# Stick-breaking attention: element-wise steps of heads, z and the last sums go from VectorE to GpSimd in quarters, and the dense filler is spread over whole blocks

## The chip, the cores and the metric

The kernel runs on one core of one Trainium2 chip. A core has five engines with queues of their own: TensorE (PE, matrix products and transposes into PSUM), VectorE (DVE), ScalarE (ACT), GpSimd (POOL, which in this kernel works on SBUF only) and SyncE (SP, which here issues DMA transfers). The metric is device time in microseconds, as the median of several runs; before the change it is 2796.8 us (three runs, 2795.46 to 2797.88).

## The reference

Two layers over a sequence of 2048 tokens with 1024 channels, all in float32. Layer 0 mixes by trailing means, then keys and values are computed once. The change lies in layer 1, which for 16 heads of 64 channels does this:

```
q, z = split(rms_norm(x) @ b_w_in)              # q normed per head
logits = q . k / 8                               # s < t only
keep   = prod over s<j<t of (1 - sigmoid(logits[t, j]))
o[t]   = sum over s of sigmoid(logits[t, s]) * keep * v[s]
x = x + (o * silu(z)) @ b_w_out
x = x + (p @ ple_w) * sigmoid(x @ ple_gate_w)
```

The kernel uses that a weight is a difference of two neighbouring products of `1 - sigmoid`: it multiplies running products with differences of v, and adds a term for the end of the block (`ends`).

## The kernel before, in words

All dense products are made from pairs: each float32 operand is split into a high part (rounded to the matmul's type) and a low part (the rest), and three matmuls per product are summed (high·high, high·low, low·high). A low part is made by one subtraction, such as line 853.

The first part of the program (to line 734) does layer 0 and k, v, q for four chunks of 512 tokens. The second part is the attention and all of layer 1's dense products.

**Attention.** The work is cut into slots `(c, h, kc)`: query chunk c from 3 down to 0, head h from 0 to 15, key chunk kc from c down to 0. That is 64, 48, 32 and 16 slots for c = 3, 2, 1, 0; "block" means the slots of one c. A slot has four steps, one for each 128 queries (or 128 keys). At step n the code calls, in this order:

- `turn` for step n − 6: four TensorE transposes of the running products into a PSUM tile `psa` (two buffers, line 799), a cast to the high part on ACT (line 802) and the low part on DVE (line 803);
- `front` for step n: two matmuls for the logits (774, 775), `1 - sigmoid` on ACT (778), on diagonal slots a mask by `affine_select` on GpSimd (780), and the running product as a scan on DVE (785);
- the filler: so many pieces of dense work as `rate` has added up to, each piece one matmul and what follows it;
- `gather` for step n − 8: two matmuls with v (811, 812). At the last step of a head it also joins the head's two partition halves: an ACT copy of one half (816) and a DVE sum (817). After every second head, four ACT instructions add `ends` (823) and GpSimd multiplies the pair of heads by silu(z) (824).

**Filler.** While c = 3 runs, the filler is `gate_z` for all four chunks: eight products of 24 matmuls each, z's normalisation on DVE (873), a sigmoid on ACT (875), a product on GpSimd (876) and a store to DRAM. While c = 2, 1, 0 run, it is `post(c + 1)`: eight output products with the residual (897), ACT's high part (899) and GpSimd's low part (900), then eight gates with sigmoid (919), product (922) and two sums (923 on GpSimd, 924 on DVE), transposes back (929), a copy (931) and the store. `pair_up` makes the high and low part of a finished pair of heads (852, 853). `post(0)` has no attention beside it; it is the tail, where `tail[0]` is set.

The rate is such that the filler of a block (`POST` pieces) is spent before the block ends:

```
POST = 8 * 24 + 8 * 30 + 9
rate = POST / (64.0 * c3 - 2 * LAG_G)      # LAG_G = 8
```

What is left when the block's heads are all there is run at once. The written order is the order of priority; a planner, which has costs of its own for the instructions, sets the final order on each engine and can move an instruction behind later ones where it takes its inputs to be late. Each engine then executes its queue in order.

Of the kernel before, what the change touches and what calls it, by code (L numbers as in the profile page):

```python
# [29 lines left out]
def f(ap):  # L30
    return ap.bitcast(F32)
# [3 lines left out]
def trunk_kernel(ctx, tc, x, p, a_norm, a_w_in, a_w_group, a_scale, a_w_out, kv_norm, w_kv,  # L35
# [143 lines left out]
    with ExitStack() as st:  # L179
# [14 lines left out]
        def tmp(nm):  # L194
            return t2.tile([P, W5], F32, tag="tmp", name=nm, bufs=8)

        halo = [[cp.tile([P, HALO], F32, name=f"halo{o}_{i}") for i in range(2)] for o in range(KT)]
        for o in range(KT):
            V.memset(halo[o][0], 0.0)

# [536 lines left out]
    with ExitStack() as st:  # L737
# [68 lines left out]
        def gather(st, kt):  # L806
            cs = slice((kt if st["diag"] else 0) * P, W5)
            if st["diag"] and kt == 0:
                st["o"].append(pso.tile([P, W5], F32, tag="pso", name="pso"))
            po, at, vv = st["o"][0], st["at"].pop(kt), st["v"]  # L810
            T.matmul(po[:, cs], vv[:, kt, :], at[:, 0, cs], start=(st["diag"] and kt == 0), stop=False)  # L811
            T.matmul(po[:, cs], vv[:, kt, :], at[:, 1, cs], start=False, stop=(st["last"] and kt == 3))  # L812
            if st["last"] and kt == 3:
                half, os, c, h2 = st["h"] % 2, st["os"], st["c"], st["h"] // 2
                mine, other = slice(half * HD, (half + 1) * HD), slice((1 - half) * HD, (2 - half) * HD)
                A.copy(out=os[mine], in_=po[other])  # L816
                V.tensor_tensor(out=os[mine], in0=po[mine], in1=os[mine], op=ALU.add)  # L817
                if half:
                    zt = t2.tile([P, W5], F32, tag="zt", name="zt", bufs=1)
                    nc.sync.dma_start(out=zt, in_=zd[c][h2])  # L820
                    for j in range(4):
                        js = slice(j * P, (j + 1) * P)
                        A.activation(out=os[:, js], in_=os[:, js], func=AF.Identity, bias=ends[c][:, h2, j : j + 1])  # L823
                    G.tensor_tensor(out=os, in0=os, in1=zt, op=ALU.mult)  # L824
                    outs[c].append(os)

        tail = [0]

        def dense():
            if tail[0] and tail[0] % 4:  # L830
# [16 lines left out]
        def pair_up(c):  # L847

            if len(ogs[c]) < len(outs[c]):
                os = outs[c][len(ogs[c])]  # L850
                pr = pair("og")
                A.copy(out=pr[:, 0], in_=os)
                V.tensor_tensor(out=pr[:, 1], in0=os, in1=f(pr[:, 0]), op=ALU.subtract)
                ogs[c].append(pr)

        def gate_z(c):

            xs = chunk[c]["x2"] if c == NSUB - 1 else []
            for o in range(len(xs), KT):
                pr = pair("xz")  # L860
                nc.sync.dma_start(out=f(pr), in_=x2p[c][o])
                xs.append(pr)
            ps = (psl if "w" in early else psa).tile([P, 4, P], F32, tag="psl" if "w" in early else "psa", name="psar")
            for j in range(4):
                T.transpose(ps[:, j, :], r2s[c][:, j : j + 1].to_broadcast([P, P]), ident)
            rb = kap.tile([P, W5], F32, tag="rb", name="rb")
            A.copy(out=rb, in_=ps.rearrange("q j t -> q (j t)"))
            for o in range(KT):
                wz = early.pop("w") if "w" in early else stored(wzd[o])
                ps = dense()  # L870
                yield from piecewise(ps, wz, xs, 0)
                zr = t2.tile([P, W5], F32, tag="tmp", name="zr", bufs=4)
                V.tensor_tensor(out=zr, in0=ps, in1=rb, op=ALU.mult)
                sg = t2.tile([P, W5], F32, tag="tmp", name="sgz", bufs=4)
                A.activation(out=sg, in_=zr, func=AF.Sigmoid)
                G.tensor_tensor(out=zr, in0=zr, in1=sg, op=ALU.mult)
                nc.sync.dma_start(out=zd[c][o], in_=zr)
                if c == 0:
                    pair_up(NSUB - 1)

        POSTZ = 8 * 24
        POST = 8 * 24 + 8 * 30 + 9

        def post(c):

# [17 lines left out]
            for k in range(2):  # L903
# [9 lines left out]
            for o in range(KT):  # L913
                wg = stored(wgd[o])
                wl = stored(wld[o])
                ps = dense()
                yield from piecewise(ps, wg, x3, 0)
                sg = t2.tile([P, W5], F32, tag="tmp", name="sg", bufs=4)
# [4 lines left out]
                (V if tail[0] else G).tensor_tensor(out=sg, in0=sg, in1=f(x3[o][:, 1]), op=ALU.add)  # L923
                V.tensor_tensor(out=sg, in0=sg, in1=f(x3[o][:, 0]), op=ALU.add)

                def finish(o=o, sg=sg):
                    pt = psa.tile([P, 4, P], F32, tag="psa", name="psao")
# [39 lines left out]
        def begin(i):  # L967
            c, h, kc = slots[i]
            if kc == c:
                if h == 1:  # L970
                    early["ends"] = load_ends(c)
                os = head["os"] if h % 2 else t2.tile([P, W5], F32, tag="os", name="os", bufs=9)
                head.clear()
                head.update(q=early.pop("q", None) or load_q(c, h), carry=[None] * 4, o=[], os=os)
            kk = early["k"].pop(0) if early["k"] else load_k(kc, h)
            active[i] = dict(head, c=c, h=h, k=kk, v=load_v(kc, h), diag=kc == c, last=kc == 0, a=[], at={})

        for n in range(4 * len(slots) + LAG_G):
# [26 lines left out]
            if 0 <= i3 < len(slots):  # L1005
                gather(active[i3], j3)
                if j3 == 3:
                    st3 = active.pop(i3)
                    c3 = st3["c"]
                    if len(outs[c3]) == 8 and c3 not in done:  # L1010
                        done.add(c3)
                        for _ in filler:
                            pass
                        if c3:
                            filler = beside(c3 - 1)
                            rate = POST / (64.0 * c3 - 2 * LAG_G)
                            owed = 0.0
        tail[0] = 1
        for _ in post(0):
# [29 lines left out]
```

## Time and profile before

| | us |
|---|---|
| median of 3 runs | 2796.8 |
| the profiled execution | 2798.39 |
| its span | 2796.3 |
| TensorE busy | 2739.2 |
| VectorE busy | 1892.1 |
| ScalarE busy | 1388.3 |
| GpSimd busy | 928.9 |
| granted TensorE clock, mean | 0.996 of full |

Terms and sums of the prediction are of the profiled execution, whose span is 2.1 us shorter than its time. A row of a group reads: line, engine, operation, output and inputs, shape, count, busy time, mean ns of one, idle time of the engine ahead of it with what ended that. A row of the waits reads: who waited for whom, us in total, times, longest. A row of the timeline reads: start, duration, instruction. TensorE's ends are modelled, so that a matmul is drawn longer than the time to the next one.

### The profile page before, as it was taken

Reading aid. Unit: us, or ns where it says so; the run is one execution under the profiler, and the core shown is the slowest. Engines: PE = TensorE matmul, PEld = TensorE weight load, DVE = VectorE, ACT = ScalarE, POOL = GpSimd, SP = SyncE. Lnnn points to the kernel's source line nnn. Section 1 sums busy time; section 2 is a strip of 40 time slices with the busy share of each in tenths; the row PEclk is TensorE's granted clock in tenths of the full one; section 3 lists DMA queues with packets and bytes.
Section 4 is the critical chain, followed back from the end, with each engine's and each line's share of the span. In section 5 each row is a group of like instructions: output and inputs, shape, how many; then the busy total and the mean of one; then the engine's idle time right before and its main releaser. Section 6 shows DMA issues by size and latency. Waiting matters only on the chain. (4 is left out here: it accounts for less than half of the span.)

```text
span 2796.3 us, 40450 instructions
## 1 busy us (share of the span) xinstructions
PE 2739.2 (98%) x13715; PEld 2265.2 (81%) x13715; DVE 1892.1 (68%) x2573; ACT 1388.3 (50%) x2801; POOL 928.9 (33%) x949
## 2 busy tenths in 40 slices
PE   9999999999999999999999999999999999999999
PEld 7878888878887888878878888887878778878877
DVE  6645634455354543545499999999999988885642
ACT  5434533355234552345356566566666665564431
POOL 2554336543475424753222112112211122213220
PEclk9999999999999999999999999999999999999999
DMA  8654696546955489444678565555555565658865
GB/s 284 239 173 160 231 315 230 181 166 220 339 194 192 157 258 315 151 145 151 196 252 276 181 222 169 170 163 185 162 162 163 183 184 183 200 181 250 256 202 161
DMA packets 335844, 573.28 MB, mean 205 GB/s; under 512 B 32463, under 2 KB 166639, under 8 KB 335637
## 3 DMA queue, kind: packets, MB, share of 16 engines
q1 hardware_dynamic: 330186, 563.03, 61.9%
q10 hardware_dynamic: 5450, 7.66, 0.9%
q8 instruction: 108, 1.77, 0.3%
q14 instruction: 100, 0.81, 0.1%
HBM read 430.01 MB, written 132.19 MB: 201 GB/s over the span
## 5 line engine op out<-in xcount | busy, mean ns | idle before, releaser
L525 PE MATMUL psd<-wpair,x 128*128 128x512 f32 x2304 | 548.4, 394 | 4.5 <-ACT x L214 3.6
L802 ACT CAST at<-psa 128x512 fp32r<-128x512 f32 (+3 forms) x640 | 333.0, 521 | 396.0 <-PE psa L799 390.3
L785 DVE TENSOR_TENSOR_SCAN pp<-kap,pp,zeros 128x512 f32<-128x512 f32 x384 | 508.0, 1324 | 5.5 <-ACT kap L778 3.9
L525 PEld LDWEIGHTS psd<-wpair,x 128*128 128x128 f32 x2304 | 429.5, 189 | 93.5 <-ACT x L214 5.0
L803 DVE TENSOR_TENSOR at<-psa,at 128x512 fp32r<-128x512 f32 (+3 forms) x640 | 379.7, 595 | 57.6 <-ACT at L802 54.9
L799 PE MATMUL psa<-ident,pp 128*128 128x128 f32 x2176 | 346.5, 275 | 21.7 <-DVE at L803 17.6
L778 ACT ACTIVATE kap<-psl 128x512 f32<-128x512 f32 (+3 forms) x640 | 343.7, 538 | 18.4 <-PE psl L775 15.1
L799 PEld LDWEIGHTS psa<-ident,pp 128*128 128x128 f32 x2176 | 263.4, 140 | 99.7 <-DVE at L803 42.2
L774 PE MATMUL psl<-kk,qa 128*128 128x512 f32 (+3 forms) x640 | 280.6, 438 | 0.7 <-ACT kap L778 0.7
L780 POOL TENSOR_SCALAR_AFFINE_SELECT kap<-kap 128x128 f32<-128x128 f32 x256 | 92.2, 361 | 558.1 <-ACT kap L778 534.7
L785 DVE TENSOR_TENSOR_SCAN pp<-kap,zeros 128x128 f32<-128x128 f32 (+3 forms) x256 | 215.9, 844 | 43.0 <-POOL kap L780 38.4
L811 PE MATMUL pso<-at,vv 128*128 128x512 f32 (+3 forms) x640 | 234.6, 367 | 1.3 <-ACT at L802 1.2
L812 PE MATMUL pso<-at,vv 128*128 128x512 f32 (+3 forms) x640 | 235.5, 368 | 0.0
L775 PE MATMUL psl<-kk,qb 128*128 128x512 f32 (+3 forms) x640 | 234.1, 366 | 0.0
L131 PE MATMUL psd<-xp,wpair 128*128 128x512 f32 x512 | 202.2, 396 | 1.7 <-ACT xp L268 1.2
L132 PE MATMUL psd<-xp,wpair 128*128 128x512 f32 x512 | 200.6, 392 | 0.0
L133 PE MATMUL psd<-xp,wpair 128*128 128x512 f32 x512 | 200.3, 391 | 0.0
L113 DVE SCALAR_TENSOR_TENSOR wpair<-wraw,gains,wpair 128x512 fp32r<-128x512 f32 x192 | 151.8, 811 | 31.2 <-ACT wpair L112 30.9
L108 POOL TENSOR_TENSOR wpair<-wraw,wpair 128x512 fp32r<-128x512 f32 x99 | 137.9, 1402 | 87.0 <-ACT wpair L106 66.8
L112 ACT ACTIVATE wpair<-wraw,gains 128x512 fp32r<-128x512 f32 x192 | 134.0, 717 | 35.4 <-PE psd L525 33.8
L811 PEld LDWEIGHTS pso<-at,vv 128*128 128x128 f32 x640 | 120.5, 188 | 28.0 <-ACT at L802 2.3
L812 PEld LDWEIGHTS pso<-at,vv 128*128 128x128 f32 x640 | 120.4, 188 | 24.7
(210 smaller groups left out, 5399.9 us busy)
## 6 DMA issues: line engine op xcount, KB each, us to landing
kk<-kd SPq DMA_DIRECT2D x320, 128.0 KB
vv<-vd SPq DMA_DIRECT2D x160, 256.0 KB
wraw<-in_w_kv_dram SPq DMA_DIRECT2D x128, 256.0 KB
wpair<-wzd SPq DMA_DIRECT2D x64, 512.0 KB
wpair<-wod SPq DMA_DIRECT2D x64, 512.0 KB
wpair<-wgd SPq DMA_DIRECT2D x64, 512.0 KB
wpair<-wu SPq DMA_DIRECT2D x48, 512.0 KB
wpair<-wi SPq DMA_DIRECT2D x36, 512.0 KB
```

The source lines that it names most:

```text
L131: T.matmul(ps, wst(units, kt, 0, c0), acts[kt][:, 0], start=(begin and kt == order[0]), stop=False)
L132: T.matmul(ps, wst(units, kt, 0, c0), acts[kt][:, 1], start=False, stop=False)
L525: T.matmul(pss2[i], ck["x2"][kt][:, xh, tk], wst(ws, kt, wh, 0, W5), start=(kt == 0 and xh == 0 and wh == 0), stop=(kt == KT - 1 and wh == 1))
L774: T.matmul(ps[:, :w], qa[:, qs], kk[:, :w], start=True, stop=False)
L775: T.matmul(ps[:, :w], qb[:, qs], kk[:, :w], start=False, stop=True)
L778: A.activation(out=kp[:, r0:], in_=ps[:, :w], func=AF.Sigmoid, scale=-1.0)
L785: V.tensor_tensor_scan(out=pp[:, r0:][:, ::-1], data0=kp[:, r0:][:, ::-1], data1=zeros.to_broadcast([P, w]), initial=1.0 if st["diag"] els ...
L799: T.transpose(pt[:, j * P : (j + 1) * P], pp[:, r0 + kt * P : r0 + (kt + 1) * P], ident)
L802: A.copy(out=at[:, 0, cs], in_=pt[:, cs])
L803: V.tensor_tensor(out=at[:, 1, cs], in0=pt[:, cs], in1=f(at[:, 0, cs]), op=ALU.subtract)
L811: T.matmul(po[:, cs], vv[:, kt, :], at[:, 0, cs], start=(st["diag"] and kt == 0), stop=False)
L812: T.matmul(po[:, cs], vv[:, kt, :], at[:, 1, cs], start=False, stop=(st["last"] and kt == 3))
```

## The change

Seven edits, all but one in the second part:

1. The halo tiles get a pool of their own that is given back when the first part ends.
2. A head's halves: ACT copies both halves out of PSUM (one to a new tile `low`, one to `os`), and GpSimd adds them, by the new function `pooled`.
3. `pooled` cuts an operation on 512 columns into four GpSimd instructions of 128 columns. In the tail, and for the last pair of heads of chunk 0, it is one instruction on VectorE.
4. The product with silu(z) and the low part of a pair of heads go through `pooled`.
5. z: ACT copies the product out of PSUM, GpSimd normalises it in quarters, and the product with the sigmoid is cut in quarters too. The low part of the residual stream (line 900) as well.
6. The last sums: high and low part of the stream are added first (`xw`, through `pooled`, ahead of the gate's matmuls), and one sum follows the gate instead of two, on GpSimd, or on VectorE in the tail.
7. The last transposes of a block's filler come six pieces later, and the rate spreads `POST` over all but four steps of a block.

```diff
-        halo = [[cp.tile([P, HALO], F32, name=f"halo{o}_{i}") for i in range(2)] for o in range(KT)]
+        hp = st.enter_context(tc.tile_pool(name="hp", bufs=1))
+        halo = [[hp.tile([P, HALO], F32, name=f"halo{o}_{i}") for i in range(2)] for o in range(KT)]
...
-                A.copy(out=os[mine], in_=po[other])
-                V.tensor_tensor(out=os[mine], in0=po[mine], in1=os[mine], op=ALU.add)
+                low = st["low"]
+                last[0] = c == 0 and h2 == NH // 2 - 1
+                A.copy(out=low[mine], in_=po[other])
+                A.copy(out=os[mine], in_=po[mine])
+                pooled(os[mine], os[mine], low[mine], ALU.add)
...
-                    G.tensor_tensor(out=os, in0=os, in1=zt, op=ALU.mult)
+                    pooled(os, os, zt, ALU.mult)
...
+        def pooled(out, in0, in1, op):
+            if tail[0] or last[0]:
+                V.tensor_tensor(out=out, in0=in0, in1=in1, op=op)
+                return
+            for j in range(4):
+                js = slice(j * P, (j + 1) * P)
+                G.tensor_tensor(out=out[:, js], in0=in0[:, js], in1=in1[:, js], op=op)
...
-                V.tensor_tensor(out=pr[:, 1], in0=os, in1=f(pr[:, 0]), op=ALU.subtract)
+                pooled(pr[:, 1], os, f(pr[:, 0]), ALU.subtract)
...
-                V.tensor_tensor(out=zr, in0=ps, in1=rb, op=ALU.mult)
+                A.copy(out=zr, in_=ps)
+                pooled(zr, zr, rb, ALU.mult)
...
-                G.tensor_tensor(out=zr, in0=zr, in1=sg, op=ALU.mult)
+                pooled(zr, zr, sg, ALU.mult)
...
-        POST = 8 * 24 + 8 * 30 + 9
+        POST = 8 * 24 + 8 * 31 + 8
...
-                G.tensor_tensor(out=pr[:, 1], in0=xr, in1=f(pr[:, 0]), op=ALU.subtract)
+                pooled(pr[:, 1], xr, f(pr[:, 0]), ALU.subtract)
...
+                xw = t2.tile([P, W5], F32, tag="tmp", name="xw", bufs=4)
+                pooled(xw, f(x3[o][:, 0]), f(x3[o][:, 1]), ALU.add)
...
-                (V if tail[0] else G).tensor_tensor(out=sg, in0=sg, in1=f(x3[o][:, 1]), op=ALU.add)
-                V.tensor_tensor(out=sg, in0=sg, in1=f(x3[o][:, 0]), op=ALU.add)
+                if tail[0]:
+                    V.tensor_tensor(out=sg, in0=sg, in1=xw, op=ALU.add)
+                else:
+                    pooled(sg, sg, xw, ALU.add)
...
+            for _ in range(6):
+                yield
             late.pop()()
...
-                            rate = POST / (64.0 * c3 - 2 * LAG_G)
+                            rate = POST / (64.0 * c3 - 4)
```

More of the change, by code (lines that the diff above doesn't have):

```diff
@@ L823, in gather @@
                         A.activation(out=os[:, js], in_=os[:, js], func=AF.Identity, bias=ends[c][:, h2, j : j + 1])
-                    G.tensor_tensor(out=os, in0=os, in1=zt, op=ALU.mult)
+                    pooled(os, os, zt, ALU.mult)
                     outs[c].append(os)
-        tail = [0]
+        def pooled(out, in0, in1, op):
[5 more added lines that the diff above has]
+                G.tensor_tensor(out=out[:, js], in0=in0[:, js], in1=in1[:, js], op=op)
+        tail, last = [0], [0]
         def dense():
@@ L972, in begin @@
                 os = head["os"] if h % 2 else t2.tile([P, W5], F32, tag="os", name="os", bufs=9)
+                low = head["low"] if h % 2 else t2.tile([P, W5], F32, tag="low", name="low", bufs=1)
                 head.clear()
-                head.update(q=early.pop("q", None) or load_q(c, h), carry=[None] * 4, o=[], os=os)
+                head.update(q=early.pop("q", None) or load_q(c, h), carry=[None] * 4, o=[], os=os, low=low)
             kk = early["k"].pop(0) if early["k"] else load_k(kc, h)
```

## The prediction

> **What bounds the kernel now.** I read the page first, then busy time by stage, then TensorE's waits, then the groups of the lines that the diff names, and last the order of events at single stalls.
>
> ```profile
> span 2796.3 us, 40450 instructions
> PE 2739.2 (98%) x13715; PEld 2265.2 (81%) x13715; DVE 1892.1 (68%) x2573; ACT 1388.3 (50%) x2801; POOL 928.9 (33%) x949
> ```
>
> TensorE (PE) is busy for all but 57 us, and the change takes no matmul away. So the gain is bounded by PE's pauses. The attention runs from 1385 us on. I cut it where the count of the sigmoids of line 778 reaches the end of a query block (256, 192, 128 and 64 of them):
>
> ```profile
> 1385.00:1885.50 500.50, 143.92 (x256) 1.00 0.64 204
> 2507.00:2684.00 177.00, 28.01 (x64) 0.99 0.79 243
> ...
> 1385.00:1886.00 501.00, 496.45 (x2704) 413.84 (x2703) 470.71 (x563) 299.39 (x598) 96.97 (x106) 1.00 0.64 204
> 1886.00:2243.00 357.00, 345.09 (x1917) 282.83 (x1916) 343.07 (x434) 227.93 (x468) 62.75 (x89) 1.00 0.55 172
> 2243.00:2506.00 263.00, 254.06 (x1401) 210.96 (x1400) 231.12 (x303) 157.02 (x336) 58.39 (x88) 1.00 0.60 188
> 2506.00:2684.00 178.00, 173.01 (x927) 145.02 (x925) 116.34 (x185) 90.16 (x214) 51.85 (x87) 0.99 0.79 243
> 2684.00:2796.30 112.30, 104.73 (x484) 85.48 (x481) 27.88 (x42) 20.93 (x40) 12.86 (x10) 0.98 0.54 171
> ```
>
> The columns after the length are busy us of PE, weight loads, VectorE (DVE), ScalarE (ACT) and GpSimd (POOL). PE's idle time is 4.6, 11.9, 8.9, 5.0 and 7.6 us (length less first column). DVE is busy for 94% of the first block, 96% of the second, 88% of the third: in the first two it is nearly a second bound. POOL is at 17 to 29%.
>
> ```profile
> 2205.00:2260.00 55.00, 48.65 (x269) 37.53 (x268) 51.46 (x66) 34.88 (x74) 9.72 (x12) 1.00 0.59 179
> 2480.00:2516.00 36.00, 31.14 (x183) 25.16 (x182) 32.79 (x44) 22.65 (x49) 7.03 (x14) 1.00 0.55 172
> ```
>
> These two stretches hold the ends of the second and third block and 6.4 + 4.9 = 11.2 us of idle PE. There the filler (the dense products that fill PE between attention steps) has run out: its rate spends 441 pieces over 64·c − 16 steps, so a block's last 16 steps have none, and PE waits for DVE.
>
> ```profile
> PE psa L799 <- DVE at L803: 17.6, 32, 1.4
> PE psao L929 <- DVE sg L924: 6.2, 4, 2.0
> ...
> DVE pp L785 <- POOL kap L780: 38.4, 62, 1.9
> ACT os L823 <- DVE os L817: 16.7, 25, 2.0
> ACT og L852 <- POOL os L824: 18.6, 17, 1.8
> ACT sgz L875 <- DVE zr L873: 13.4, 17, 2.6
> ```
>
> The wait that ends last is line 799's: the transposes need a PSUM buffer that DVE's subtraction (line 803) has yet to read. One stall in order of time:
>
> ```profile
> 2216.74 1.33 POOL L824 TENSOR_TENSOR os<-os,zt 128x512 f32<-128x512 f32 x1 [9.83 <-ACT os L823]
> 2217.34 1.82 DVE L785 TENSOR_TENSOR_SCAN pp<-kap,pp,zeros 128x512 f32<-128x512 f32 x1 [0.16 <-ACT kap L778]
> 2218.65 0.39 PE L840 MATMUL psd<-x,wpair 128*128 128x512 f32 x1
> 2218.88 0.39 PE L842 MATMUL psd<-x,wpair 128*128 128x512 f32 x1
> 2219.08 0.66 DVE L853 TENSOR_TENSOR og<-os,og 128x512 fp32r<-128x512 f32 x1
> 2219.66 0.68 DVE L803 TENSOR_TENSOR at<-psa,at 128x512 fp32r<-128x512 f32 x1
> 2220.26 1.27 DVE L785 TENSOR_TENSOR_SCAN pp<-kap,pp,zeros 128x512 f32<-128x512 f32 x1
> 2220.40 0.66 PE L799 MATMUL psa<-ident,pp 128*128 128x128 f32 x4 [0.95 <-DVE at L803]
> ```
>
> The scan beside GpSimd's product takes 1.82 us instead of 1.27, line 853 stands ahead of line 803, and PE stops for 0.95 us. Matmuls start 0.23 us apart but are drawn 0.39 long, so each stall hides 0.16 us more: 32 × 0.16 = 5 us.
>
> **The change part by part.**
>
> ```profile
> L785 DVE TENSOR_TENSOR_SCAN pp<-kap,pp,zeros 128x512 f32<-128x512 f32 x384 | 508.0, 1324 | 5.5 <-ACT kap L778 3.9
> L817 DVE TENSOR_TENSOR os<-pso,os 64x512 f32<-64x512 f32 x64 | 43.5, 680 | 6.6 <-ACT os L816 5.5
> L853 DVE TENSOR_TENSOR og<-os,og 128x512 fp32r<-128x512 f32 x32 | 22.7, 716 | 8.9 <-ACT og L852 8.9
> L873 DVE TENSOR_TENSOR zr<-psd,rb 128x512 f32<-128x512 f32 x32 | 21.4, 667 | 0.4 <-PE psd L844 0.4
> L924 DVE TENSOR_TENSOR sg<-sg,x 128x512 f32<-128x512 f32 x32 | 25.9, 808 | 21.8 <-POOL sg L923 21.5
> L816 ACT COPY os<-pso 64x512 f32<-64x512 f32 x64 | 37.1, 580 | 31.6 <-PE pso L812 31.2
> L824 POOL TENSOR_TENSOR os<-os,zt 128x512 f32<-128x512 f32 x32 | 43.4, 1355 | 136.7 <-ACT os L823 136.5
> L876 POOL TENSOR_TENSOR zr<-zr,sgz 128x512 f32<-128x512 f32 x32 | 60.4, 1886 | 212.4 <-issue 136.7 <-ACT sgz L875 43.8 <-DVE at L803 19.5
> L780 POOL TENSOR_SCALAR_AFFINE_SELECT kap<-kap 128x128 f32<-128x128 f32 x256 | 92.2, 361 | 558.1 <-ACT kap L778 534.7 <-DVE pp L785 8.7 <-DVE at L803 8.5
> ```
>
> *Vector time removed.* Head sums 62 × 0.68 = 42 us (the last pair stays on DVE), low parts about 31 × 0.716 = 22, z's norm 32 × 0.667 = 21, last sums 24 × 0.808 = 19: 104 us over four blocks. The second block loses 16 × 0.68 + 8 × 0.716 + 8 × 0.808 = 23 us of its 343.
>
> *GpSimd time added.* No row shows a two-input 128x128 product. From below I take the select's 0.361 (one input, same size), from above a quarter of 1.886, 0.47. I use 0.42, nearer the upper end because the op has two inputs like that row: 1.68 us for four. 62 + 32 + 31 + 24 = 149 new products make 250 us, and the 111 whole products already there (lines 824, 876, 900, 923) change little. Block shares: the second gets 32 × 1.68 = 54 us, so POOL goes from 63 to 117 of 357; the last about as much, from 52 to 106 of 178.
> By the Trainium skill, "GPSIMD Engine Reference", § Performance versus the Vector engine, an add of 2048 elements is measured at 4497 ns; in proportion that gives an estimate of 0.28 us for a quarter and 167 us for the 149, which would return some 6 us less of Vector time below. No run here shows a quarter yet.
>
> *What DVE pays back.* Its 384 full scans average 1.324 instead of 1.27, 20 us lost beside about 270 us of GpSimd work (the POOL column summed over the four blocks): 0.07 us per us. 250 us more cost 18 us. Net relief 86 us, in the second block 23 − 4 = 19, which takes DVE there from 96% to 93% of a block shortened by 9 us.
>
> *ScalarE.* 62 more head copies and 32 of z at 0.58: 55 us on an engine that is 51 to 64% busy. They lie beside PE, and they free a head's PSUM after two copies (1.16 us) where a copy and a Vector sum took 1.26. More important are waits in its queue: the sigmoid of z waited 13.4 us in all for one Vector product, and will wait for four quarters, 1.68 instead of 0.667, 1.0 us more each time; behind it stand the casts of line 802 and sigmoids of line 778. What covers this: a cast has until the buffer's next turn two steps on, 2 × 501/256 = 3.9 us, less the cast (0.59, taken as the copy's 0.58) and the subtraction 0.68, so 2.6 us. A wait of 1.7 fits; without the cover each excess us falls on PE. The biases of line 823 go by quarters behind the quarter sums, so they start after one quarter, about as now after 0.68. z's store then stands about 2 us longer at the head of SP's queue, with k and v loads behind it; these are asked for a slot of four steps (7.8 us) ahead, which covers it, and without that cover PE would wait for k. No DMA is added. The select of line 780 queues behind quarters as it did behind whole products; DVE's 38.4 us of waits for it stay as they are within bounds of ± 10, in blocks where DVE has that room.
>
> *The spread.* 448 pieces over 64·c − 4 steps: 2.38 instead of 2.51 a step in the second block, 3.61 instead of 3.94, 7.47 instead of 9.19. The gap shrinks from 16 to 4 steps. The same matmuls are done, so what is saved is the idle time of the gaps: of 11.2 us about three quarters, 8.5 (bounds: 4 if DVE still sets those steps, 13 with the hidden part).
>
> *Stalls inside the blocks.* The first three have 25.4 − 11.2 = 14 us of idle PE there, with hidden ones nearly 18. The relief takes a share; I take half, 9 (bounds 0 and 18). The six idle pieces before a block's last finish belong here: line 929 waited 6.2 us in four places, three of them before the tail.
>
> *Last block and tail.* 5.0 us idle, PE-bound with more filler than it needs; I take 2 (bounds −8, from the third rival below, and 5). In the tail everything is Vector again, with one addition less behind the last product. That saves nothing at the end:
>
> ```profile
> 2789.45 0.58 ACT L931 COPY ot<-psao 128x512 f32<-128x512 f32 x1 [1.28 <-PE psao L929]
> 2791.33 0.63 PE L929 MATMUL psao<-ident,sg 128*128 128x128 f32 x4 [1.96 <-DVE sg L924]
> 2792.46 0.58 ACT L931 COPY ot<-psao 128x512 f32<-128x512 f32 x1 [2.42 <-DMA out_dram<-ot]
> ```
>
> the last copy waits for the single output buffer's earlier transfer, not for the sum. The halo tiles' new pool costs nothing: it moves addresses.
>
> *Sum.* 8.5 + 9 + 2 less 1.5 for waits on ACT that outgrow the cover (bounds 0 and the first rival's 34): 18 us off the profiled span of 2796.3, 2778.3. That execution took 2798.39, 2.1 more than its span and 1.6 above the median of 2796.8. So 2796.8 − 18 = 2779.
>
> **The rivals.**
>
> *GpSimd holds ScalarE's queue (slower).* The evidence for it is one select:
>
> ```profile
> 2244.04 1.47 POOL L780 TENSOR_SCALAR_AFFINE_SELECT kap<-kap 128x128 f32<-128x128 f32 x1 [13.34 <-ACT kap L778]
> ```
>
> 1.11 us longer than the mean select, as if a scan had to pass first. If z's four quarters let two scans pass, they take 4 × 0.36 + 2 × 1.11 = 3.7 us; ACT's sigmoid waits that long, 1.1 beyond the cover, in each of 32 gates: 34 us, against 9 us of gains that remain. Time 2796.8 + 25 = 2822. It decides from 2.6 us for four quarters on. Against it: one whole product under scans took 1.886 on average, and the scans leave 0.7 us gaps of 1.96.
> The Trainium skill, "SBUF — State Buffer", § Who interferes with whom, has it so: a Vector instruction with two SBUF inputs and a GpSimd one that reads SBUF exclude each other for a whole instruction. The trace agrees in part: the scan above grew by 0.55 us where 0.73 of it lay beside the product.
>
> *Vector wasn't what PE waited for.* The relief turns into waits of DVE for ACT; only about half of the gaps' 8.5 comes: 2792. For it: PE's named waits for line 803 are 17.6 us of 1411. Against: the 94 and 96%.
>
> *GpSimd binds the last block.* At four steps there (178/16 = 11 us) it would have four selects, and in the gate part four quartered products: 1.4 + 4 × 1.68 = 8.2 us, fits; from 0.6 us a quarter it doesn't, and half of 16 such groups lose 1 us: 8 us, 2787.
>
> *More comes.* All stalls and hidden parts go: 13 + 18 + 5 = 36 us, 2761.
>
> **How the numbers follow.** Forecast 0.48, more 0.12, no limit 0.14, GpSimd in the last block 0.08, slower 0.18. 0.2% is 5.6 us, about what can be told from no change. The third case splits 0.05 faster, 0.07 same, 0.02 slower; the fourth 0.06 and 0.02; the slower rival 0.16 slower, 0.02 same. Faster 0.71, same 0.11, slower 0.18. The range reaches from 2758 to 2803, a quarter of the way to the slower rival; the forecast's own is 2768 to 2788.
>
> **What would show it.** Right: idle PE at the two block ends falls from 11.2 to under 4 us; waits of line 799 for 803 fall to under 9 us; DVE in the second block under 95%; quarters of 0.36 to 0.47 us. Wrong: quarters above 0.65 us, ACT waits for GpSimd above 60 us with PE waiting for casts or sigmoids, or line 799's waits unchanged.

## The result and the profile after

The change makes the kernel slower: 2865.66 us (median of six runs, 2859.2 to 2868.68) against 2797.34 (six runs); the ratio is 1.0242, 95% interval 1.0229 to 1.0255. The forecast was 18 us less. 68 us more came.

First the changed kernel's page, then its busy time by stage, cut at the same steps as in the prediction (the ends of the four blocks, then the tail). Fences of waits and groups show only the rows that the text uses.

```profile
span 2863.8 us, 41200 instructions
PE 2763.1 (96%) x13715; PEld 2274.6 (79%) x13715; DVE 1818.1 (63%) x2433; ACT 1440.6 (50%) x2897; POOL 1362.5 (48%) x1869
```

```profile
1385.00:1928.00 543.00, 513.88 (x2708) 419.68 (x2707) 440.70 (x511) 322.01 (x646) 273.60 (x433) 0.98 0.60 188
1928.00:2297.00 369.00, 345.63 (x1906) 283.15 (x1905) 327.12 (x401) 235.85 (x482) 182.18 (x292) 1.00 0.51 161
2297.00:2572.00 275.00, 260.35 (x1412) 214.65 (x1410) 211.26 (x276) 169.07 (x355) 136.55 (x284) 0.99 0.61 185
2572.00:2745.00 173.00, 165.64 (x891) 139.41 (x890) 99.93 (x148) 96.64 (x224) 120.68 (x280) 0.99 0.76 236
2745.00:2863.80 118.80, 111.73 (x518) 90.89 (x516) 34.49 (x52) 24.35 (x46) 5.40 (x13) 0.99 0.58 187
```

The first part of the program is unchanged (the attention starts at 1385 us in both). The first block takes 543 us where it took 501, the second and third 12 us more each. The last block and the tail must be read together, since the spread moves the border between them: 291.8 us instead of 290.3. Vector did become freer, 441 instead of 471 us in the first block. But TensorE idles 29 us there where it idled 4.6, and is drawn busy for 17 us more, with the granted clock at 0.98. GpSimd, the last of the busy columns, is far above what was forecast: 182 us in the second block instead of 117.

The changed kernel's waits in the whole trace (line 800 is the former 799, 804 the former 803, 786 the scan, 781 the mask, 890 the sigmoid of z, 827 the biases):

```profile
DVE pp L786 <- POOL kap L781: 150.5, 109, 5.2
DVE at L804 <- ACT at L803: 98.2, 141, 3.5
ACT sgz L890 <- POOL zr L839: 56.1, 30, 4.4
PE psa L800 <- DVE at L804: 53.9, 67, 2.9
ACT os L827 <- POOL os L839: 25.8, 28, 2.6
```

TensorE's wait for the subtraction has tripled (17.6 before). Behind it stand Vector's waits, for ScalarE's casts (54.9 before) and for GpSimd's masks (38.4 before), and ScalarE's waits for GpSimd's quarters. The groups of the quarters say why:

```profile
L839 POOL TENSOR_TENSOR os<-os,low 64x128 f32<-64x128 f32 x248 | 156.3, 660 | 194.1 <-ACT os L820 186.1 <-DMA qa<-qd 7.4
L839 POOL TENSOR_TENSOR zr<-zr,rb 128x128 f32<-128x128 f32 x128 | 82.8, 676 | 85.2 <-ACT zr L887 85.2
```

A quarter takes 0.66 to 0.68 us on average in these groups, not 0.42. And this is what one pause looks like, on the changed kernel's timeline:

```profile
1600.14 1.23 DVE L786 TENSOR_TENSOR_SCAN pp<-kap,zeros 128x512 f32<-128x512 f32 x1 [0.17 <-POOL kap L781]
...
1600.30 2.57 POOL L839 TENSOR_TENSOR zr<-zr,rb 128x128 f32<-128x128 f32 x4 [0.20 <-ACT zr L887]
...
1602.90 0.63 ACT L890 ACTIVATE sgz<-zr 128x512 f32<-128x512 f32 x1 [1.59 <-POOL zr L839]
...
1603.44 0.58 ACT L779 ACTIVATE kap<-psl 128x512 f32<-128x512 f32 x1
...
1604.05 1.52 DVE L786 TENSOR_TENSOR_SCAN pp<-kap,pp,zeros 128x512 f32<-128x512 f32 x1 [2.02 <-ACT kap L779]
```

The scan starts just ahead of the four quarters, which take 2.57 us from the first's start to the last's end. ScalarE stands for 1.59 us at z's sigmoid. The next step's sigmoid of the logits (779), whose input has long been there, is behind it in the queue, and Vector stands for 2.02 us until that sigmoid has come and the scan can start. TensorE doesn't stop at this one, since its transposes are six steps behind the scans; but Vector, busy for 94% of this block before the change, has little time to make such pauses up. That TensorE runs dry after several of them is a reading of the order of events; the test is the run with z's part put back, below. A longer pause of TensorE can be followed by a stretch at half the clock. In this one ScalarE had waited 3.47 us for a GpSimd product left over from the first part (line 599), which stood behind z's quarters; at the same place the kernel before pauses for 1.38 us:

```profile
1412.96 1.10 PE L800 MATMUL psa<-ident,pp 128*128 128x128 f32 x4 [2.35 <-DVE at L804]
```

```profile
1413.00:1416.40 3.40, 3.40 (x10) 2.85 (x11) 3.40 (x5) 1.33 (x3) 0.00 (x0) 0.50 0.88 256
```

(the last three columns of a window are granted clock, DMA share and GB/s). By the two pages TensorE is idle for 43.6 us more than before (100.7 instead of 57.1) and drawn busy for 23.9 us more. The mean granted clock of the whole run is 0.991 of 2863.8 us against 0.996 of 2796.3, so about 25.8 − 11.2 = 15 us more of clock were not granted. This is a consequence of the pauses and at most a part of the loss: z's part alone, below, cost 36 us with a granted clock of 0.998 in its profiled execution.

### The profile page after: what moved, and what is told of

Read it like the earlier page. It is cut to its first block, busy times and chain, and to the rows that moved or that the text cites. A ratio compares the mean times of both kernels' runs of the same rounds, so it can differ in the third digit from the quotient of the medians.

```text
span 2863.8 us, 41200 instructions
## 1 busy us (share of the span) xinstructions
PE 2763.1 (96%) x13715; PEld 2274.6 (79%) x13715; DVE 1818.1 (63%) x2433; ACT 1440.6 (50%) x2897; POOL 1362.5 (48%) x1869
## 3 DMA queue, kind: packets, MB, share of 16 engines
q1 hardware_dynamic: 330186, 563.03, 60.4%
## 5 line engine op out<-in xcount | busy, mean ns | idle before, releaser
L786 DVE TENSOR_TENSOR_SCAN pp<-kap,pp,zeros 128x512 f32<-128x512 f32 x384 | 510.2, 1329 | 31.3 <-ACT kap L779 29.5
L804 DVE TENSOR_TENSOR at<-psa,at 128x512 fp32r<-128x512 f32 (+3 forms) x640 | 377.3, 590 | 99.2 <-ACT at L803 98.2
L800 PE MATMUL psa<-ident,pp 128*128 128x128 f32 x2176 | 352.7, 278 | 62.3 <-DVE at L804 53.9
L786 DVE TENSOR_TENSOR_SCAN pp<-kap,zeros 128x128 f32<-128x128 f32 (+3 forms) x256 | 229.4, 897 | 152.1 <-POOL kap L781 150.5
L839 POOL TENSOR_TENSOR os<-os,low 64x128 f32<-64x128 f32 x248 | 156.3, 660 | 194.1 <-ACT os L820 186.1
L781 POOL TENSOR_SCALAR_AFFINE_SELECT kap<-kap 128x128 f32<-128x128 f32 x256 | 84.9, 340 | 217.7 <-ACT kap L779 207.1
L812 PEld LDWEIGHTS pso<-at,vv 128*128 128x128 f32 x640 | 121.5, 190 | 27.7 <-ACT at L803 0.5
```

Of the source, the lines that this page charges most:

```text
L786: V.tensor_tensor_scan(out=pp[:, r0:][:, ::-1], data0=kp[:, r0:][:, ::-1], data1=zeros.to_broadcast([P, w]), initial=1.0 if st["diag"] els ...
L800: T.transpose(pt[:, j * P : (j + 1) * P], pp[:, r0 + kt * P : r0 + (kt + 1) * P], ident)
L804: V.tensor_tensor(out=at[:, 1, cs], in0=pt[:, cs], in1=f(at[:, 0, cs]), op=ALU.subtract)
L839: G.tensor_tensor(out=out[:, js], in0=in0[:, js], in1=in1[:, js], op=op)
```

## The experiments

The kernel before was timed again beside them, with medians of 2798.7 to 2800.3 us; ratios below are to it. Four of the eleven take one part of the change alone, three undo or vary one part of it, one takes away what was suspected to hold GpSimd up, and three look for what is worth keeping.

**The spread alone.**

```diff
-        POST = 8 * 24 + 8 * 30 + 9
+        POST = 8 * 24 + 8 * 31 + 8
...
+            for _ in range(6):
+                yield
             late.pop()()
...
-                            rate = POST / (64.0 * c3 - 2 * LAG_G)
+                            rate = POST / (64.0 * c3 - 4)
```

> The kernel before with the seventh edit alone: the rate over 64c - 4 steps, POST of 448 pieces, six idle pieces ahead of a block's last finish. No work moves to GpSimd. The prediction's term for the block ends expects 8.5 us less (2789; bounds 4 to 13), with idle PE at the ends of the second and third block falling from 11.2 to under 4 us. The rival, that Vector sets those steps whatever the filler does, expects 2797 within 3. If the spread itself were a cause of the loss, the time would be above 2803.

Measured: 2789.29 us, ratio 0.9967 (0.9956 to 0.9979). Windows of this kernel at the ends of its second and third block:

```profile
2205.00:2260.00 55.00, 51.69 (x293) 42.34 (x292) 53.22 (x67) 35.88 (x76) 7.12 (x12) 1.00 0.59 177
2475.00:2511.00 36.00, 33.71 (x191) 27.88 (x189) 32.20 (x43) 21.64 (x48) 7.87 (x13) 1.00 0.68 192
```

Idle TensorE there is 3.3 + 2.3 = 5.6 us instead of 11.2. The spread is a gain, as big as forecast, and no part of the loss. Block by block it is less neat: the second block's idle time as a whole stayed (12.4 us, 11.9 before), the third's fell from 8.9 to 6.1, and the last block with the tail took 285 us instead of 290.

**z's part put back.** The changed kernel, with this:

```diff
-                A.copy(out=zr, in_=ps)
-                pooled(zr, zr, rb, ALU.mult)
+                V.tensor_tensor(out=zr, in0=ps, in1=rb, op=ALU.mult)
...
-                pooled(zr, zr, sg, ALU.mult)
+                G.tensor_tensor(out=zr, in0=zr, in1=sg, op=ALU.mult)
```

> The changed kernel, with z's normalisation back on Vector (one instruction out of PSUM) and the product with the sigmoid back in one GpSimd instruction. Theory A (ScalarE's queue: the sigmoid of z waits for GpSimd quarters that a scan holds up, and casts stand behind it) expects the first block to lose most of its 42 us excess (543 to about 510) and the total to fall by 30 or more, to about 2830. Theory B (masks queue behind quarters on GpSimd and the scans wait) expects at most 10 us off, since 19 of 109 such waits lie in the first block: above 2850.

Measured: 2828.35 us, 1.0103 (1.0089 to 1.0117): 37 us less than with z's part. The first block of this kernel:

```profile
1385.00:1887.50 502.50, 494.28 (x2682) 410.70 (x2681) 459.41 (x539) 305.83 (x608) 169.02 (x213) 1.00 0.66 203
```

TensorE's idle time in it is 8.2 us instead of 29.1. The attention starts 5 us earlier in this execution (1380.7 us), so the block's length is better taken from its first to its last sigmoid of the logits: 505.4 us against 541.3 with the change and 499.7 before. So 36 of the first block's 42 us are gone. Theory A holds there; what is left, 29 us against the kernel before, lies mostly in the later blocks.

**The mask on Vector.** The changed kernel, with this:

```diff
-                G.affine_select(out=kp[:, W5 - P :], in_=kp[:, W5 - P :], pattern=[[-1, P]], compare_op=ALU.is_gt,
-                                fill=1.0, base=0, channel_multiplier=1)
+                V.tensor_tensor(out=kp[:, W5 - P :], in0=kp[:, W5 - P :], in1=mask, op=ALU.max)
```

(`mask` is a constant tile, made once.)

> The changed kernel with the diagonal mask made on Vector (a maximum with a constant tile) instead of GpSimd's select: no scan waits for GpSimd any more; Vector gets 256 instructions of some 0.3 us, 75 us. Theory B expects the 150 us of waits of scans for the mask to vanish, and the excess of the second to fourth block (12 + 10 + 3 us) with a part of the first's to go: about 2835. Theory A expects the first block to stay near 543 and the total within 10 of 2866.

Measured: 2845.38 us, 1.0166 (1.015 to 1.0181), 20 us less than the change. The scans' waits for the mask are gone, but the other waits stay (rows of this kernel, where 893 is z's sigmoid and 830 the biases):

```profile
ACT sgz L893 <- POOL zr L842: 62.5, 32, 4.4
PE psa L803 <- DVE at L807: 41.3, 53, 3.4
ACT os L830 <- POOL os L842: 26.9, 28, 2.5
```

The masks themselves now take 88 us of Vector's time (256 of 0.345 us). The blocks tell where the 20 us went. Lengths in us, from one block's last sigmoid of the logits to the next block's (the first block from its first one):

| | first | second | third | last |
|---|---|---|---|---|
| kernel before | 499.7 | 357.5 | 263.2 | 173.6 |
| spread alone | 499.9 | 358.6 | 259.1 | 163.6 |
| the change | 541.3 | 369.8 | 273.3 | 170.8 |
| z's part put back | 505.4 | 369.3 | 271.8 | 171.3 |
| mask on Vector | 533.1 | 376.3 | 261.4 | 164.4 |

With the mask on Vector the third and the last block are back within 3 us of the spread alone, although ScalarE waits for the biases as before. There theory B holds. In the first block the mask accounts for 8 of 41 us, and the second got 6.5 us longer, with Vector's added work in it. So theory B is a part, and a smaller one than its 150 us of waits suggested.

**Whole pieces.** The changed kernel, with this:

```diff
-            for j in range(4):
-                js = slice(j * P, (j + 1) * P)
-                G.tensor_tensor(out=out[:, js], in0=in0[:, js], in1=in1[:, js], op=op)
+            G.tensor_tensor(out=out, in0=in0, in1=in1, op=op)
```

> The changed kernel with each moved operation in one GpSimd instruction of 512 columns in place of four of 128. Theory Q (the quarters are the loss: each of four can be made to let a scan of 1.3 us pass, 222 of 1044 were) expects fewer and shorter total holds, one per operation, and a time between 2800 and 2840. Theory M (moving the work to GpSimd at all is the loss) expects 2860 or more, since a mask then queues behind 1.3 to 2 us at a time and the biases of the heads wait for the whole sum.

Measured: 2824.04 us, 1.009 (1.0073 to 1.0107), 42 us less than with quarters. Groups and waits of this kernel:

```profile
L837 POOL TENSOR_TENSOR zr<-zr,rb 128x512 f32<-128x512 f32 x32 | 53.5, 1673 | 118.0 <-ACT zr L885 118.0
L837 POOL TENSOR_TENSOR os<-os,low 64x512 f32<-64x512 f32 x62 | 92.8, 1497 | 224.3 <-ACT os L820 214.1 <-DMA qa<-qd 7.4 <-ACT at L803 2.3
```

```profile
DVE pp L786 <- POOL kap L781: 98.0, 105, 3.1
ACT os L827 <- POOL os L837: 32.3, 31, 3.7
ACT sgz L888 <- POOL zr L837: 24.4, 27, 1.8
```

z's product takes 1.67 us in one piece; in four it takes 82.8 / 32 = 2.59 us, the busy time of its group over 32 products (a quarter starts shortly before the one ahead ends, so this is less than 4 × 0.676). The wait of its sigmoid falls from 56 to 24 us, that of the masks from 150 to 98, and only the biases wait longer (32 instead of 26), since they no longer start on the first quarter. Theory Q holds for 42 us; 35 us against the spread alone remain for the move itself.

**One part alone.** Three kernels are the kernel before with one part of the change each, not spread: z's part, the heads (copies, sum and product with silu(z), here in the tail too), and the low parts with the last sums (on Vector in the tail).

```diff
-                V.tensor_tensor(out=zr, in0=ps, in1=rb, op=ALU.mult)
+                A.copy(out=zr, in_=ps)
+                pooled(zr, zr, rb, ALU.mult)
...
-                G.tensor_tensor(out=zr, in0=zr, in1=sg, op=ALU.mult)
+                pooled(zr, zr, sg, ALU.mult)
```

> The kernel before with z's part alone: copy out of PSUM on ScalarE, normalisation and product with the sigmoid on GpSimd in quarters. All in the first block. Theory A (the sigmoid waits in ScalarE's queue for quarters that scans hold up) expects what taking it out of the changed kernel gave, 30 to 40 us more: about 2832, with the first block near 535 instead of 501, the sigmoid's waits for GpSimd 50 us or more, and stretches of halved TensorE clock in the first block only. If the 37 us came from the parts together, it is below 2815.

```diff
-                A.copy(out=os[mine], in_=po[other])
-                V.tensor_tensor(out=os[mine], in0=po[mine], in1=os[mine], op=ALU.add)
+                low = st["low"]
+                A.copy(out=low[mine], in_=po[other])
+                A.copy(out=os[mine], in_=po[mine])
+                pooled(os[mine], os[mine], low[mine], ALU.add)
...
-                    G.tensor_tensor(out=os, in0=os, in1=zt, op=ALU.mult)
+                    pooled(os, os, zt, ALU.mult)
```

> The kernel before with the head sums alone (two copies on ScalarE, sum on GpSimd in quarters) and the product with silu(z) in quarters. Vector loses 43 us of work. The prediction's theory (Vector's relief is worth about half of what it frees in stalls) expects 2790 to 2797. Theory B (masks queue behind quarters) and theory A at the biases (line 823 waits for quarters) expect 2805 to 2825, with the scans' waits for the mask at 60 us or more instead of 38.

```diff
-                V.tensor_tensor(out=pr[:, 1], in0=os, in1=f(pr[:, 0]), op=ALU.subtract)
+                pooled(pr[:, 1], os, f(pr[:, 0]), ALU.subtract)
...
-                G.tensor_tensor(out=pr[:, 1], in0=xr, in1=f(pr[:, 0]), op=ALU.subtract)
+                pooled(pr[:, 1], xr, f(pr[:, 0]), ALU.subtract)
...
+                xw = t2.tile([P, W5], F32, tag="tmp", name="xw", bufs=4)
+                pooled(xw, f(x3[o][:, 0]), f(x3[o][:, 1]), ALU.add)
...
-                (V if tail[0] else G).tensor_tensor(out=sg, in0=sg, in1=f(x3[o][:, 1]), op=ALU.add)
-                V.tensor_tensor(out=sg, in0=sg, in1=f(x3[o][:, 0]), op=ALU.add)
+                pooled(sg, sg, xw, ALU.add)
```

> The kernel before with the low parts of heads and of the residual stream and the last sums on GpSimd in quarters, one Vector sum less. Nothing on ScalarE waits for these quarters except later casts, so theory A expects 2797 within 5. Theory B expects 2805 to 2820, most of it in the second and third block, with the scans' waits for the mask at 70 us or more. The prediction's theory expects 2788 to 2795.

Measured, beside 2798.67 us:

| alone | us | ratio, 95% interval |
|---|---|---|
| z's part | 2834.97 | 1.0124 (1.0108 to 1.0139) |
| heads | 2836.14 | 1.0128 (1.0113 to 1.0143) |
| low parts and last sums | 2802.62 | 1.0016 (1.0006 to 1.0026) |

With the spread's −10 these are +36, +37 and +4, together 67: the change's 68, so the parts nearly add up. The heads cost more than any theory expected of them (2825 at most), and the low parts lie at the upper edge of theory A's 2797 within 5. Waits of two of these kernels, first the heads', then the low parts':

```profile
DVE pp L786 <- POOL kap L781: 75.8, 78, 2.1
PE psa L800 <- DVE at L804: 33.4, 47, 2.0
ACT os L826 <- POOL os L833: 23.5, 29, 1.9
```

```profile
DVE pp L785 <- POOL kap L780: 90.4, 98, 3.7
PE psa L799 <- DVE at L803: 19.9, 34, 1.5
```

The low parts make the masks wait most (90 us) and cost almost nothing. The heads make them wait less and cost ten times as much. What differs is ScalarE: the biases stand in its queue for GpSimd, as z's sigmoid does, and casts and sigmoids of the logits stand behind them. So the main cost in the first two blocks seems to be GpSimd's time where ScalarE waits for it in order. For z's part two runs show the size (put back, and alone) and the timeline shows the way; for the heads the way is argued from the waits. Masks that delay only a scan are mostly hidden in the kernel with the low parts alone, but with the whole change they are the loss of the third and the last block, as the run with the mask on Vector shows. How the heads' 37 us divide between biases, masks and the extra copies was not tried.

**What holds a quarter up.** The scan reads two tensors from SBUF: the keep factors and a broadcast column of zeros. This kernel is the changed one with the sigmoid of the logits written back over the logits in PSUM, so that the scan reads one tensor from SBUF; the mask is made in place by Vector, since GpSimd works on SBUF only here.

```diff
-            A.activation(out=kp[:, r0:], in_=ps[:, :w], func=AF.Sigmoid, scale=-1.0)
+            A.activation(out=ps[:, :w], in_=ps[:, :w], func=AF.Sigmoid, scale=-1.0)
...
+                V.tensor_tensor(out=ps[:, w - P : w], in0=ps[:, w - P : w], in1=mask, op=ALU.max)
...
-                V.tensor_tensor_scan(out=pp[:, r0:][:, ::-1], data0=kp[:, r0:][:, ::-1],
+                V.tensor_tensor_scan(out=pp[:, r0:][:, ::-1], data0=ps[:, :w][:, ::-1],
```

> The changed kernel with the sigmoid of the logits written back into PSUM: the scan then reads one tensor from PSUM and only the zeros from SBUF; the mask is made there by Vector. If a scan with two SBUF inputs is what holds the quarters up, no quarter outside other two-input Vector instructions takes 1.3 us any more (222 of 1044 did, now under 40), four quarters take 1.8 us, the sigmoid of z waits 25 us or less instead of 56, and the time falls well below 2845, what the mask on Vector alone gave: 2800 to 2825. If quarters are held up by something else, they stay as they are and the time is 2840 or more. Against it: PSUM buffers of the logits stay taken until the scan has read them, and TensorE may wait for them.

Measured: 2791.25 us, 0.997 (0.9957 to 0.9983), below the 2800 to 2825 that were expected: 54 us less than with the mask on Vector and the scan's input in SBUF, 74 less than the change. Its groups (787 is the scan, 840 the quarters) and the wait of z's sigmoid:

```profile
L787 DVE TENSOR_TENSOR_SCAN pp<-psl,pp,zeros 128x512 f32<-128x512 f32 x384 | 489.9, 1276 | 24.1 <-ACT psl L781 22.2
L840 POOL TENSOR_TENSOR os<-os,low 64x128 f32<-64x128 f32 x248 | 106.2, 457 | 299.5 <-ACT os L821 299.1
L840 POOL TENSOR_TENSOR zr<-zr,rb 128x128 f32<-128x128 f32 x128 | 54.9, 460 | 259.9 <-ACT zr L888 259.9
```

```profile
ACT sgz L891 <- POOL zr L840: 27.6, 31, 1.9
```

Counted one by one, 218 of the changed kernel's 1040 quarters took over 0.8 us, mostly 1.37 (the 222 of 1044 in the expectations have four whole products among them). Each of the 218 lies over a scan and ends 0.24 to 0.27 us after that scan's end. Now none does; a quarter takes 0.46 us everywhere and the scan 1.276, as it does alone. What held them up was the scan's second input from SBUF. That it isn't the shorter scan that gives the 54 us is shown by the next section: the same edit gives 3 to 5 us where nothing is moved. This bears out the Trainium skill's "SBUF — State Buffer", § Who interferes with whom: a Vector instruction with two SBUF inputs keeps a GpSimd instruction that reads SBUF out, one with a single SBUF input doesn't.

**What is worth keeping.** Three more kernels have the scan's input in PSUM. The first is the last kernel with z's part as before:

```diff
-                A.copy(out=zr, in_=ps)
-                pooled(zr, zr, rb, ALU.mult)
+                V.tensor_tensor(out=zr, in0=ps, in1=rb, op=ALU.mult)
...
-                pooled(zr, zr, sg, ALU.mult)
+                G.tensor_tensor(out=zr, in0=zr, in1=sg, op=ALU.mult)
```

> The changed kernel with the sigmoid of the logits and the mask in PSUM, and z's part as before (normalised by Vector, one product on GpSimd). The first block was 509 us with z on GpSimd in quarters and no blocked quarter, against 500 with the spread alone: theory A's queue (27.6 us of the sigmoid's waits are left) expects these 9 us back: 2782 within 3. If the 9 us are Vector's mask and not the queue, the time stays at 2791.

The second is the kernel before with the spread, the scan's input in PSUM, and nothing moved to GpSimd:

```diff
-            A.activation(out=kp[:, r0:], in_=ps[:, :w], func=AF.Sigmoid, scale=-1.0)
+            A.activation(out=ps[:, :w], in_=ps[:, :w], func=AF.Sigmoid, scale=-1.0)
...
+                V.tensor_tensor(out=ps[:, w - P : w], in0=ps[:, w - P : w], in1=mask, op=ALU.max)
...
-                V.tensor_tensor_scan(out=pp[:, r0:][:, ::-1], data0=kp[:, r0:][:, ::-1],
+                V.tensor_tensor_scan(out=pp[:, r0:][:, ::-1], data0=ps[:, :w][:, ::-1],
```

> The spread alone, with the sigmoid of the logits and the mask in PSUM: nothing is moved to GpSimd. It tells what the moves are worth once no scan holds GpSimd up. If Vector's relief is worth anything, this is slower than with the moves of heads, low parts and sums: 2788 to 2800, because Vector has 75 us of masks more, less 25 us of shorter scans. If it is worth nothing, it equals or beats the run with z's part put back.

The third is the whole change with the scan's input in PSUM and whole pieces:

```diff
-            for j in range(4):
-                js = slice(j * P, (j + 1) * P)
-                G.tensor_tensor(out=out[:, js], in0=in0[:, js], in1=in1[:, js], op=op)
+            G.tensor_tensor(out=out, in0=in0, in1=in1, op=op)
```

> The changed kernel with the sigmoid of the logits and the mask in PSUM and whole GpSimd instructions in place of quarters. Unblocked, a whole one takes 1.28 us and four quarters 1.70. With whole ones the sigmoid of z waits less, the biases of the heads longer: 2784 to 2791 if the queue at the sigmoid counts, 2791 or more if the biases do.

Measured, beside 2800.29 us:

| scan's input in PSUM, with | us | ratio, 95% interval |
|---|---|---|
| the change without z's part | 2781.13 | 0.9936 (0.9924 to 0.9949) |
| the spread alone | 2786.57 | 0.995 (0.9939 to 0.9962) |
| the whole change, whole pieces | 2787.86 | 0.9959 (0.9945 to 0.9973) |
| the whole change, quarters (above) | 2791.25 | 0.997 (0.9957 to 0.9983) |

The first beats both the kernel before and the changed one. Its first two blocks:

```profile
1385.00:1885.00 500.00, 497.97 (x2705) 414.76 (x2704) 464.34 (x607) 306.00 (x612) 94.41 (x151) 1.00 0.65 205
1885.00:2240.00 355.00, 349.34 (x1925) 286.38 (x1924) 338.08 (x473) 236.05 (x487) 96.12 (x225) 1.00 0.56 168
```

TensorE idles 2.0 and 5.7 us in them (4.6 and 11.9 before the change). z's part costs 10 us even with no quarter held up: the queue at its sigmoid (27.6 us of waits) is the likeliest remainder. Whole pieces and quarters can't be told apart there, since their intervals overlap. What heads, low parts and sums are worth on GpSimd, once nothing holds it up, is about 5 us: 2781.13 against 2786.57, with intervals that overlap. And the scan's input in PSUM by itself, with nothing moved, is worth 3 us by the medians (2786.57 against 2789.29 for the spread alone) and 5 by the ratios, again with intervals that overlap.

## Why the prediction was wrong

**Right.** What bounds the kernel (TensorE, paused by line 803) and the gap at the block ends: the spread alone gave 10 us where the term said 8.5. The idle time there fell to 5.6 us, not under 4, and the second block as a whole lost none of its idle time, so that the sum came out so near is in part luck. Vector's relief came, too: 1189 us from 1385 us to the end fell to 1114, by 75 (86 were forecast). It was worth nothing here, since the waits took it back: the scans' for the sigmoid of the logits alone went from 3.9 to 29.5 us.

**The step that failed: the price of four quarters and what it waits for.** The text took 0.42 us a quarter, 1.68 for four, from a row of whole products. Unhindered it is 0.46. Held up by a scan it is 1.37, and every quarter can be held up anew. The means of 0.66 and 0.68 lie above both ends that were given (0.361 and 0.47): the upper one divided a whole product's hindrance by four, where one hindrance falls on one quarter. The row that showed it stood in the prediction, the select of 1.47 us, but it was used for a rival only. The products already on GpSimd, put at "change little", were cut too and grew: z's with the sigmoid took 60.4 us in 32 pieces and 76.9 in quarters. An estimate from the Trainium skill's "GPSIMD Engine Reference", § Performance versus the Vector engine, in proportion to length, was 0.28 us; the measurement decides, and part of an instruction's time doesn't shrink with its length: with the scan's input in PSUM a whole one takes 1.28 to 1.29 us, not 4 × 0.46.

**The second step that failed: the cover of ScalarE's waits.** 2.6 us were worked out for the cast of line 802, from the two buffers of the transposes. But the sigmoid of the logits stands in the same queue, and the scan of the same step takes it up at once: there the cover is nothing. The sum had 1.5 us for waits that outgrow the cover; z's part alone cost 36. In the timeline above 1.59 us of ScalarE's wait became 2.02 of Vector's. That fits z's part costing 36 us though its four quarters took 2.59 us on average, no more than the cover.

**The third: the masks.** "Within bounds of ± 10" was 38.4 to 150.5 us. The size was far off; the price of it was about 20 us, by the run with the mask on Vector, which also paid 88 us of Vector's time for it.

**The rivals.** The slower one named the right place and mechanism: z's sigmoid behind quarters that scans hold up. Its sum for z's part was 34 us, and alone it cost 36, but that is luck: it put the four quarters at 3.7 us, 1.1 beyond the cover, and they took 2.59. What it left out is that heads have the same queue (their biases, in a part that cost 37 us), so it said 2822 where 2866 came.

The Trainium skill's rule beside it ("SBUF — State Buffer", § Who interferes with whom) was the better guide to the price than the row of whole products, and the trace before bore it out more fully than "in part". The scan that grew by 0.55 us ended 1.09 us after the product's end; alone it takes 1.27, so for most of the 0.73 us beside the product it stood still. The other way, 61 of the 120 products of lines 824, 876, 900 and 923 started while a scan ran, and each ended 1.06 to 1.17 us after the scan's end, where an unhindered one takes 1.28. For line 876 the shortest, median and longest product took 1.277, 2.068 and 3.774 us. From such rows the length of one hold could have been read.

"Vector wasn't what PE waited for" had its waits right: Vector's waits for ScalarE's casts rose from 54.9 to 98.2 us. It priced them only as half of the block ends' gain, which came in full (10 us). The relief is worth about 5 us where nothing holds GpSimd up.

"GpSimd binds the last block" came, by another way. That block's 173 us (178 before) hide it, since the spread alone shortens the block: by the table above the change's is 7.2 us longer than the spread's, and the rival said 8 from 0.6 us a quarter on. But GpSimd was busy for only 120.7 of the 173 us. The scans waited 57.8 us there for masks behind quarters, and with the mask on Vector the block is as short as with the spread alone (164.4 and 163.6).

**The end of the program.** The saved Vector sum gave nothing, as said. The end of the changed kernel's timeline:

```profile
2857.75 0.63 PE L948 MATMUL psao<-ident,sg 128*128 128x128 f32 x4 [1.24 <-DVE sg L941]
...
2859.60 0.59 ACT L950 COPY ot<-psao 128x512 f32<-128x512 f32 x1 [2.42 <-DMA out_dram<-ot]
```

TensorE waits 1.24 us for the sum instead of 1.96, and the last copy waits 2.42 us for the transfer before, as it did.

## What to carry to other kernels

A slower engine with free time takes work off a busy one only where nobody stands in an ordered queue for its result: count, for each moved instruction, who waits for it in order and what stands behind that, and take the smallest cover among those, not the one of the path you had in mind. Cutting an instruction in pieces multiplies the chances of being held up, so price a piece by the longest hindrance in the trace, not by a share of the mean. And look for the second SBUF input of the long Vector instructions before work goes to GpSimd beside them: moving one input to PSUM took away 54 us of this change's loss, though with nothing moved it was worth only 3 to 5.

## What the runs showed of the hardware

- A quarter (128x128, two inputs) on GpSimd takes 0.46 us alone, and mostly about 1.37 when a scan of 1.27 us was running: it waits, it isn't slowed, since all 218 held quarters end 0.24 to 0.27 us after a scan's end. The scan's inputs are the keep factors and a column of zeros broadcast over the free dimension. With the factors in PSUM and the zeros still in SBUF the hindrance is gone in all 1040 quarters, so the zeros count as one of the two SBUF inputs. The subtraction of line 804, with one input from PSUM and one from SBUF, holds none: about 290 quarters of the changed kernel started beside it and weren't held. (The other case, with the zeros elsewhere and the factors in SBUF, was not run.)
- Between 1385 and 2600 us of the changed kernel, TensorE's granted clock fell to half nine times, for 3.4 us or twice that. Seven of these stretches began within 1.5 us of the end of a pause that the trace draws as 1.88 to 2.88 us long (2.35 us ahead of the one at 1413 us). But pauses of 2.33 us (at 1448 us) and 2.94 us (at 2179 us) had none behind them.
- ScalarE reads and writes the same PSUM tile in place at the old pace (128x512 in 0.587 us, 0.602 into SBUF), and the scan from PSUM takes 1.276 us, as from SBUF (1.27).
